# Two entries in an order-writer's clock: when a transfer may first be read, and what GpSimd's powers cost

## The chip, the cores and the metric

The kernel runs on one core of a Trainium2 chip. The metric is the device time of one execution in microseconds (us). Three runs of the kernel before took 699.75, 700.22 and 701.14 us; the median is 700.22 us.

## The reference

One decoder layer for 512 tokens of width 1024, in float32. A vector `c` gives six modulation vectors, shift, scale and gate for each of two sublayers:

```
h = x * (1 + sc1) + sh1
proj = h @ w_in                      # q, k, v (8 heads x 64), z, xBC, dt
o_attn = block-sparse causal attention(q, k, v) with ALiBi
xs, B, C = split(silu(conv4(xBC)))   # 16 heads x 64, 2 groups, state 128
dt = softplus(dt_raw + bias);  a = -exp(a_log)
y = ssd_scan(xs, dt, a, B, C) + xs * d      # chunks with cumulative sums of dt * a
y = rmsnorm_by_group(y * silu(z)) * norm_w
x = layer_norm(alpha * x + (1 + g1) * (concat(o_attn, y) @ w_out))
h = x * (1 + sc2) + sh2
u = conv3(h @ w_up);  y = (silu(u[:2816]) * u[2816:]) @ w_down
x = layer_norm(alpha * x + (1 + g2) * y)
```

The scan needs, for each head and each chunk of tokens, the matrix exp(cs[l] - cs[s]) for l >= s, where cs is the running sum of dt * a. These running sums are the "decay sums" of this document. The layer norms and the grouped norm need a power of -0.5 of a variance.

## The kernel before, in words

Tokens lie in four tiles of 128. Every float32 product is three products of a rounded part and its remainder (`mm3`, line 456): weights arrive by DMA as `raw`, ScalarE (ACT) rounds them to `wh`, VectorE (DVE) subtracts and gives `wl`. Modulation and the first product (`first`) come at the start, then the input projection (`fm` with features on the partitions, `tm` for the values with tokens on them), with the state-space scan and the attention woven in, then the output projection `po` with the first layer norm (LN1), the up projection (`up`, and from the fourth pair of tiles on a scheme of seven half-size products, `sP`), the down projection `dn` and the second layer norm (LN2).

Nothing of the order is written by hand. The work is written as some dozens of generators, called threads here. Each yields one operation, or a list of TensorE operations, or a request for a buffer, or a condition. `Order.run` (line 356) holds a model clock for each engine and each DMA queue. Again and again it asks for each thread's next operation when it could start by this clock, takes the earliest (within 0.2 us of it, on the vector engines, the one of best priority) and emits it into its engine's queue. On the chip, every engine then works through its queue in that order, and waits for what an instruction needs. The clock therefore changes nothing but the order; a wrong clock leaves engines waiting with ready work behind the waiting instruction.

Three places of the clock matter:

* `price` (line 198) gives the duration of an operation on an engine. For GpSimd's power it takes a constant and a term for each column (line 230).
* `start` (line 240) gives the earliest start: the end of each write that is read, a latency by the writing engine (`LAT`, line 237; 1.0 us for SP, which issues the DMAs), a margin for TensorE of 0.35 us, and a number `late` of the buffer, which is added only where its last writer was a DMA of SP:

```
t = max(t, w[0] + self.LAT[w[1]] + margin + (r.late if w[1] == "S" else 0.0))
```

* `emit` (line 275) moves the clocks on. A DMA of SP is issued 0.47 us (0.64 with 64 partitions) after the one before it, and lands no earlier than 0.65 us after that, plus its size over 350 GB/s or, with short runs, a larger figure; transfers follow one another.

`try_alloc` (line 146) sets `late` when it hands out a buffer, by the buffer's name.

The decay sums take this way. `dt_chain` (line 856) makes the running sums of all 16 heads, writes them transposed to DRAM (`drcs`, line 903), and negated to `ncs`. For each of eight units of two heads `ssd_decay` (line 943) then takes a buffer `csb` (three at a time) and reads 4 KB of the sums into all 128 partitions at once, 512 KB:

```
yield S.dma_start(c_.rearrange("p t h l -> p (t h l)"), bass.AP(tensor=cs_d.tensor, ...))   # 947
...
yield A.activation(er[q], c_[q, 1:, i], AF.Exp)            # 953, twice: the first use
yield G.affine_select(c_, c_, ... fill=NEG)                # 956
yield A.activation(c_[:, t, h], c_[:, t, h], AF.Exp, bias=ncs[...])   # 960, eight times
yield V.tensor_mul(q, q, b)                                # 965, twice
```

`er` is on 64 partitions each. `ssd_out` (line 997) multiplies the result with the values on TensorE (`py`). Beside it `ssd_state` (line 969) makes the chunk states: a product `pst`, a copy of its first chunk to `st` on ACT or DVE, updates of `st` on DVE, and a product `pyo`, which is multiplied with `er`. Convolutions of the input (`conv4`, line 815) use ACT too, with a tanh written to `th`.

The powers are GpSimd's (POOL's) `tensor_tensor` with `half`, which holds -0.5: one of four columns for each of the two groups in `norm` (line 1210, tile `ss`), and one of a single column for each token tile of LN1 and of LN2 in `ln_stats` (line 1248, tile `mv`). In LN1 (`ln1`, line 1269) DVE then makes the bias, ACT and DVE write one half each of the normalised rows `XN`, and TensorE transposes these (`pt`). LN2's last tile is `ln2` with `last` set (line 1474).

Of the kernel before, what the change touches and what calls it, by code (L numbers as in the profile page):

```python
# [32 lines left out]
def _n(ap):  # L33
    n = 1
    for d in ap.shape[1:]:
        n *= d
    return n
# [70 lines left out]
class Order:  # L108
# [37 lines left out]
    def try_alloc(self, a):  # L146
        if a.after:
            if self.due(a) > self.time:
                return None
            a.after = ()  # L150
        pool, slots = self.pools[a.cls]
        group = a.group or a.cls
        if self.used.get(group, 0) >= self.quota.get(group, 1000):
            return None
        free = [s for s in slots if s["free"]]
        if not free:
            return None
        s = min(free, key=lambda q: q["end"])
        t = pool.tile(a.shape, a.dt, name=self.name(a.name), tag=s["tag"], bufs=1)
        s["free"] = False  # L160
        self.used[group] = self.used.get(group, 0) + 1
        self.regs[t.tensor.name] = Region(s["end"])
        self.regs[t.tensor.name].psum = a.cls == "ps"
        self.regs[t.tensor.name].whole = a.name == "sP"
        self.regs[t.tensor.name].late = 2.0 if a.name == "ad" else 0.0
        self.owner[t.tensor.name] = (s, group)
        return t

# [29 lines left out]
    def price(self, eng, fn, outs, ins, kw):  # L198
        n = max(_n(a) for a in outs + ins)
        if eng == "PE":  # L200
            if fn == "transpose":
                return 0.109
            lhs, rhs = ins[0], ins[1]
            cols, m = _n(rhs), _n(lhs)
            if lhs.dtype == F32R:
                return max(0.111 if m > 64 else 0.056, cols * 0.0004557)
            return max(0.222, cols * 0.00168) if m > 64 else 0.000834 * cols
        if eng == "GD":
            run = 512 if any(a.tensor.name.startswith("in_") for a in ins) else 2048
            return 4 * P * _n(outs[0]) / run * (0.02 + 9.0e-5 * run) / 16  # L210
        if eng == "S":
            size = 4
            for d in outs[0].shape:
                size *= d
            ap = [a.ap for a in outs + ins if a.tensor.name.startswith(("in_", "out_", "dr"))][-1]
            run = 4 * (ap[-1][1] if ap[-1][0] == 1 else 1)
            return max(size / 3.5e5, size / run * (0.007 + 4.0e-5 * run) / 16)
        ptr = sum(1 for a in ins if _n(a) == 1)
        if eng == "A":
            return 0.04 + 0.00093 * n + (0.06 + 0.07 * ptr if ptr else 0) + (0.09 if "accum_out" in kw else 0)  # L220
        if eng == "V":
            if fn == "reciprocal":
                return 0.065 + 0.0065 * n
            if fn in ("tensor_scalar", "tensor_copy") and all(a.space != PSUM for a in ins):
                return 0.065 + 0.00052 * n + (0.06 if ptr else 0)
            return 0.065 + 0.00104 * n + (0.06 if ptr else 0)
        if fn in ("affine_select", "memset", "iota"):
            return 0.06 + 0.001 * n + (0.5 if n > 512 else 0)
        if kw.get("op") == OP.pow:
            return 0.3 + 0.164 * n  # L230
        if fn == "scalar_tensor_tensor":
            return 0.1 + 0.00139 * n
        if fn in ("tensor_scalar", "tensor_copy"):
            return 0.12 + 0.0034 * n
        return 0.1 + 0.0022 * n
# [1624 lines left out]
```

## Time and profile before

| | |
|---|---|
| timed runs, us | 699.75, 700.22, 701.14 |
| median, us | 700.22 |
| span of the profiled execution, first to last instruction, us | 698.5 |
| TensorE busy, of the span | 684.3 us, 98% |
| VectorE, ScalarE, GpSimd busy | 87%, 56%, 15% |
| mean granted TensorE clock | 0.997 |
| moved by DMA | 116.64 MB |

The profile gives no other time of the profiled execution than its span; the median of the timed runs is 1.7 us more. In the rows of a timeline stand the start, the duration, the engine, the operation with what it writes and reads, and in brackets how long the engine had been idle before and what ended that. Nearly all operations carry line 309, where the order-writer emits them, so rows are told apart by their tiles. A timed busy share of TensorE includes the tails of pipelined products; the distance from one start to the next tells more.

### The profile page before, as it was taken

To read this page: it belongs to the slowest core of one execution; us is meant where nothing else is said; L and a number is where in the kernel's file an instruction comes from. 1 tells how busy PE (TensorE), PEld (TensorE's weight loads), DVE (VectorE), ACT (ScalarE), POOL (GpSimd) and SP (SyncE) were. 2 spreads that over 40 slices of the span, in tenths; PEclk is the share of its full clock that TensorE was granted. 3 is DMA by queue.
4 is the path that set the end of the run, shared out by engine and by line. 5 is a ranking of instruction groups with operands and counts; after the bars stand their busy time and mean duration, and the time that the engine had idled before them with its cause. 6 is when DMAs were issued, how large, how long until landed. Compare 5 with 4: busy or idle time off the path is not lost.

```text
span 698.5 us, 11597 instructions
## 1 busy us (share of the span) xinstructions
PE 684.3 (98%) x4305; PEld 598.0 (86%) x4305; DVE 607.3 (87%) x1119; ACT 387.8 (56%) x739; POOL 103.4 (15%) x109
## 2 busy tenths in 40 slices
PE   8999999999999999999999999999999999999995
PEld 7787877888888888887898999999999998888885
DVE  5888989899999999889999999999999997357646
ACT  2437568845667545313886777777777776111300
POOL 0010021101000000000121121112222005910023
PEclk9999999999999999999999999999999999999998
DMA  8997074134455626677493787877897576232202
GB/s 269 308 289 241 16 215 149 37 87 126 120 178 160 237 92 212 246 275 256 137 233 73 174 200 165 187 174 167 189 204 173 130 255 220 94 108 70 91 30 92
DMA packets 134924, 116.64 MB, mean 167 GB/s; under 512 B 4565, under 2 KB 113489, under 8 KB 134867
## 3 DMA queue, kind: packets, MB, share of 16 engines
q1 hardware_dynamic: 122099, 105.93, 49.4%
q0 software_dynamic: 12768, 9.96, 9.8%
q8 instruction: 34, 0.56, 0.3%
q14 instruction: 23, 0.19, 0.1%
HBM read 106.66 MB, written 4.23 MB: 159 GB/s over the span
## 4 chain that ended last, share of the span: by engine, by line
PE 85%; DVE 6%; DMA 4%; SPq 3%; ACT 1%; issue 1%; POOL 0%; DVEq 0%; ACTq 0%; POOLq 0%
PE sP L309 27%; PE fm L309 18%; PE dn L309 18%; PE po L309 7%; PE first L309 3%; SPq L309 3%; PE tm L309 2%; PE psS L309 2%; PE pov L309 1%; PE pT L309 1%; PE py L309 1%; DMA csb<-drcs 1%; PE pyo L309 1%; PE up L309 1%; DMA raw<-in_ffn_up_w_dram 1%
## 5 line engine op out<-in xcount | busy, mean ns | idle before, releaser
L309 PE MATMUL sP<-ts,wq 128*128 128x256 f32 x912 | 113.9, 281 | 0.0
L309 DVE TENSOR_TENSOR wl<-raw,wh 128x1024 fp32r<-128x1024 f32 x64 | 80.6, 1265 | 36.6 <-ACT wh L309 36.1
L309 ACT ACTIVATE wh<-raw 128x1024 fp32r<-128x1024 f32 x64 | 67.3, 1055 | 78.0 <-PE dn L309 31.1
L309 PEld LDWEIGHTS sP<-ts,wq 128*128 128x128 f32 x912 | 110.4, 189 | 0.0
L309 PE MATMUL dn<-wh,mid 128*128 128x512 f32 (+1 forms) x356 | 102.7, 371 | 0.0
L309 PE MATMUL sP<-h2h,wq 128*128 128x256 f32 x456 | 87.2, 281 | 0.0
L309 PEld LDWEIGHTS dn<-wh,mid 128*128 128x128 f32 x356 | 64.7, 188 | 12.6
L309 PEld LDWEIGHTS sP<-h2h,wq 128*128 128x128 f32 x456 | 72.7, 189 | 0.0
L309 PE MATMUL fm<-hh,wh 128*128 128x512 f32 x176 | 72.6, 412 | 0.0
L309 PE MATMUL fm<-hh,wl 128*128 128x512 f32 x176 | 69.4, 394 | 0.0
L309 PE MATMUL fm<-hl,wh 128*128 128x512 f32 x176 | 69.4, 394 | 0.0
L309 PE MATMUL dn<-wl,mid 128*128 128x512 f32 (+1 forms) x178 | 66.1, 372 | 0.0
L309 PE MATMUL sP<-h2l,wq 128*128 128x256 f32 x228 | 64.0, 281 | 0.0
L309 DVE TENSOR_TENSOR wq<-raw,wq 128x512 fp32r<-128x512 f32 x76 | 50.8, 686 | 0.7
L309 ACT ACTIVATE wq<-raw 128x512 fp32r<-128x512 f32 x76 | 45.3, 623 | 0.0
L309 ACT ACTIVATE c<-sP 128x256 f32<-128x256 f32 x76 | 29.0, 382 | 28.5 <-PE sP L309 28.2
L309 PEld LDWEIGHTS sP<-h2l,wq 128*128 128x128 f32 x228 | 43.1, 189 | 0.1
L309 PE MATMUL po<-wh,os 128*128 128x512 f32 x128 | 42.1, 396 | 0.0
L309 PEld LDWEIGHTS fm<-hh,wl 128*128 128x128 f32 x176 | 33.1, 188 | 7.7
L309 PEld LDWEIGHTS fm<-hh,wh 128*128 128x128 f32 x176 | 33.2, 189 | 7.0 <-issue 0.7
L309 DVE TENSOR_TENSOR wq<-sw,wq 128x512 fp32r<-128x512 f32 x57 | 38.8, 684 | 0.0
L309 PEld LDWEIGHTS dn<-wl,mid 128*128 128x128 f32 x178 | 33.5, 188 | 6.2
(264 smaller groups left out, 1489.9 us busy)
## 6 DMA issues: line engine op xcount, KB each, us to landing
raw<-in_ffn_up_w_dram SPq DMA_DIRECT2D x44, 512.0 KB, 4.5
raw<-in_mix_in_w_dram SPq DMA_DIRECT2D x26, 512.0 KB, 5.8
ad<-in_ada_w_dram SPq DMA_DIRECT2D x24, 512.0 KB, 3.9
raw<-in_ffn_down_w_dram SPq DMA_DIRECT2D x22, 512.0 KB, 3.7
aw<-in_ada_w_dram SPq DMA_DIRECT2D x32, 256.0 KB, 5.8
raw<-in_mix_out_w_dram SPq DMA_DIRECT2D x12, 512.0 KB, 4.0
sw<-in_ffn_up_w_dram SPq DMA_DIRECT2D x19, 256.0 KB, 4.9
raw<-raw POOLq DMA_DIRECT2D x19, 256.0 KB, 4.6
```

What stands on the lines that cost most here:

```text
L309: getattr(self.hw[op.eng], op.fn)(*op.args, **op.kw)
```

## The change

In `try_alloc`, buffers named `csb` get a `late` of 3.0 us; so far only `ad` had one, 2.0 us. In `price`, a power on GpSimd with n columns costs 0.78 + 0.1 n us instead of 0.3 + 0.164 n: for one column 0.88 instead of 0.464, for four 1.18 instead of 0.956.

```diff
-        self.regs[t.tensor.name].late = 2.0 if a.name == "ad" else 0.0
+        self.regs[t.tensor.name].late = {"ad": 2.0, "csb": 3.0}.get(a.name, 0.0)
...
         if kw.get("op") == OP.pow:
-            return 0.3 + 0.164 * n
+            return 0.78 + 0.1 * n
```

No operation, buffer or transfer is added or taken away. What changes is the order in which the queues are filled.

## The prediction

> **What bounds the kernel now.** I read the engine shares first, then busy time by stage, then what TensorE waited for, and last the timelines around the two edited places.
>
> ```profile
> span 698.5 us, 11597 instructions
> PE 684.3 (98%) x4305; PEld 598.0 (86%) x4305; DVE 607.3 (87%) x1119; ACT 387.8 (56%) x739; POOL 103.4 (15%) x109
> ```
>
> TensorE is busy for 98% of the span, so a new order of the same work can gain only what TensorE still waits. By stage (the window, its length, then busy time of PE, PEld, DVE, ACT and POOL with counts, granted clock, DMA share, GB/s):
>
> ```profile
> 60.00:90.00 30.00, 30.00 (x149) 23.65 (x148) 28.11 (x59) 16.32 (x30) 0.00 (x0) 1.00 0.20 58
> 90.00:126.00 36.00, 34.66 (x223) 28.21 (x222) 31.14 (x56) 27.71 (x68) 7.36 (x6) 1.00 0.63 192
> 126.00:268.00 142.00, 141.99 (x845) 116.47 (x844) 134.72 (x322) 86.50 (x191) 8.38 (x14) 1.00 0.41 127
> 268.00:343.00 75.00, 74.28 (x358) 60.12 (x357) 66.27 (x111) 29.66 (x49) 3.28 (x4) 1.00 0.67 232
> 343.00:381.00 38.00, 37.95 (x273) 35.36 (x272) 36.24 (x57) 30.09 (x55) 7.67 (x7) 1.00 0.77 180
> 381.00:568.00 187.00, 187.00 (x1584) 187.00 (x1584) 185.44 (x301) 138.47 (x265) 34.99 (x32) 1.00 0.78 177
> 568.00:691.00 123.00, 123.00 (x597) 102.56 (x595) 75.27 (x93) 32.72 (x43) 36.17 (x25) 1.00 0.34 114
> ```
>
> Between 60 and 691 us TensorE is idle for 1.34 us in 90 to 126, for 0.72 us in 268 to 343, and for 0.06 us elsewhere. The waits of the window 60 to 381 name the places (total, times, longest):
>
> ```profile
> PE pyo L309 <- ACT st L309: 0.8, 1, 0.8
> PE pt L309 <- DVE XN L309: 0.7, 2, 0.4
> PE py L309 <- issue: 0.5, 1, 0.5
> ```
>
> The first and third lie where the decay sums come back from DRAM, the second in LN1, where GpSimd raises the variance to -0.5. The change edits the planned times of just these two things. Everything before 88 us, where neither occurs, should stay as it is.
>
> **The change part by part.** No instruction and no DMA is added or removed. Only the build-time clock moves, and with it the order in each engine's queue.
>
> *The decay sums.* ACT's timeline at the first use:
>
> ```profile
> 90.92 1.05 ACT L309 ACTIVATE wh<-raw 128x1024 fp32r<-128x1024 f32 x1
> 95.51 1.07 ACT L309 ACTIVATE er<-csb 64x384 f32<-64x384 f32 x2 [3.54 <-DMA csb<-drcs]
> 96.61 0.63 ACT L309 ACTIVATE th<-Y 128x512 f32<-128x512 f32 x1
> 98.24 1.07 ACT L309 ACTIVATE er<-csb 64x384 f32<-64x384 f32 x2 [1.00 <-DMA csb<-drcs]
> 99.33 0.28 ACT L309 ACTIVATE st<-pst 128x128 f32<-128x128 f32 x1
> 99.63 1.06 ACT L309 ACTIVATE wh<-raw 128x1024 fp32r<-128x1024 f32 x1
> 100.59 1.05 ACT L309 ACTIVATE er<-csb 64x384 f32<-64x384 f32 x2
> 101.67 7.14 ACT L309 ACTIVATE csb<-csb,ncs 128x128 f32<-128x128 f32 x24
> ...
> 90.42 1.39 SPq L309 DMA_DIRECT2D csb<-drcs  x3
> ```
>
> Three transfers are issued from 90.42 us. The first is usable 95.51 - 90.42 = 5.1 us later and the second 2.73 us after it. The order's clock (lines 278 to 281 and LAT at 237) gives a free queue 0.47 + 0.65 + 1.50 + 1.0 = 3.6 us, and 1.50 us for each next one. So `er` stands in ACT's queue 1.5 us too early, or more, and ACT waits 3.54 and 1.00 us with `th` and `st` queued behind it. `st` copies a state product out of PSUM, and TensorE's `pyo` waits for it:
>
> ```profile
> 98.42 0.39 PE L309 MATMUL tm<-wh,hl 128*128 128x512 f32 x1
> 99.66 1.38 PE L309 MATMUL pyo<-CT,st 128*128 128x128 f32 x6 [0.85 <-ACT st L309]
> 100.79 0.48 PE L309 MATMUL tm<-wh,hh 128*128 128x512 f32 x1
> ...
> 151.30 0.83 PE L309 MATMUL pyo<-CT,st 128*128 128x128 f32 x6
> 151.88 0.48 PE L309 MATMUL fm<-hh,wh 128*128 128x512 f32 x1
> ```
>
> From start to start an undisturbed `pyo` takes 151.88 - 151.30 = 0.58 us and a `tm` product 0.23. Here both took 100.79 - 98.42 = 2.37 us, so 1.56 us is lost: the idle 0.85, and six products that follow the four small `st` updates on VectorE one by one. With 3.0 us added, the clock gives 6.6, 8.1 and 9.6 us after 90.42, against the trace's 5.1, 7.8 and (no wait) at most 10.2. All three then stand about where the data is, and `th` and `st` move ahead. Between nothing and 1.56 us I take **1.40**, near the upper end, because the wait that held `st` is named in the rows.
>
> The Trainium skill weighs in here: "DMA: Bandwidth & Descriptors", section "Anatomy of one DMA", fits one transfer as about 2.0 us plus bytes over 436 GB/s, an estimate of 3.2 us for these 512 KB. By that the old clock was late enough, the 3.0 us would be pure delay, and the sum would lose its 1.40. The trace has 5.1 us and a wait of 3.54, and I go by the trace.
>
> A further loss is a `py` behind VectorE's backlog:
>
> ```profile
> 110.82 0.40 PE L309 MATMUL tm<-wh,hl 128*128 128x512 f32 x1
> 111.69 1.09 PE L309 MATMUL py<-csb,xd 128*64 128x128 f32 x16 [0.47 <-issue]
> ...
> 106.23 0.40 PE L309 MATMUL tm<-wh,hl 128*128 128x512 f32 x1
> 106.56 0.66 PE L309 MATMUL py<-csb,xd 128*64 128x128 f32 x8
> ```
>
> 0.87 us from `tm` to `py`, against 0.33 at an undisturbed place: 0.54 lost. It may go with the late chain or recur elsewhere; I take half, **0.27**.
>
> What is late next: per unit two `er` (1.07 us), a GpSimd select, eight exps and two VectorE products, then `py`. They may come up to 3.0 us later in the plan. The cover is the value projection and the products after it: 126 to 268 us shows 0.01 us of TensorE idle. Its price is nothing while that lasts, and up to 3.0 us without it. The later five transfers get the 3.0 us too, but their rows show no wait for the DMA, so nothing is to be gained there.
>
> *The powers.* The clock priced one column at 0.3 + 0.164 = 0.46 us and four at 0.96; now it is 0.88 and 1.18.
>
> ```profile
> L309 POOL TENSOR_TENSOR mv<-mv,half 128x1 f32<-128x1 f32 x8 | 7.1, 886 | 137.0 <-DVE mv L309 130.6 <-ACT acch L309 6.4
> L309 POOL TENSOR_TENSOR ss<-ss,half 128x4 f32<-128x4 f32 x2 | 2.4, 1187 | 72.3 <-DVE ss L309 72.3
> ...
> 327.45 0.55 POOL L309 TENSOR_TENSOR mv<-mv,half 128x1 f32<-128x1 f32 x1 [51.72 <-DVE mv L309]
> 333.20 0.87 POOL L309 TENSOR_TENSOR mv<-mv,half 128x1 f32<-128x1 f32 x1 [5.20 <-DVE mv L309]
> ...
> 328.62 0.40 PE L309 MATMUL po<-wh,oa 128*128 128x512 f32 x1
> 329.43 1.09 PE L309 MATMUL pt<-ident,XN 128*128 128x128 f32 x8 [0.41 <-DVE XN L309]
> ...
> 334.30 0.39 PE L309 MATMUL po<-wh,os 128*128 128x512 f32 x1
> 334.99 0.30 PE L309 MATMUL pt<-ident,XN 128*128 128x128 f32 x1 [0.31 <-DVE XN L309]
> ```
>
> Means of 0.886 and 1.187 agree with the new prices. In LN1 the normalised rows `XN`, and behind them the transposes `pt`, were planned 0.42 us early. The two waits cost 0.81 + 0.69 - 2 x 0.23 = 1.04 us of TensorE. The first pow took only 0.55, so its error was 0.09; correcting 0.09 + 0.42 is worth some 0.5. I take **0.40**, between nothing and 1.04. The four-column powers are 0.22 us later behind a full TensorE: nothing. LN2's last pow comes after the last product, inside one thread whose own order can't change: nothing, and at most 0.3 either way.
>
> *New waits of the reshuffled order.* Every later choice can flip. The bounds are nothing and all of today's idle over again, 2.1 us; I take **0.30**, near the lower end, as the longest stretch with a free choice (126 to 268) shows 0.01.
>
> Sum: 1.40 + 0.27 + 0.40 - 0.30 = 1.77 us. The span goes from 698.5 to 696.7. The median of the runs, 700.22, stands 1.7 us above that one span, which I keep: **698.5 us**.
>
> **The rivals.** *All of it goes:* 1.56 + 0.54 + 1.04 = 3.1 us, 697.1. For it: these are all the waits there are. Against: it needs no new one in 600 us.
>
> *The wait only moves:* ACT still has three `er` pairs and 24 exps for the first three units, and `py` follows them; if TensorE loses there what it gains at 99 us, only the powers' share stays, 699.9. For it: from 98.24 us on ACT's rows follow one another without a gap, and the exps alone take 7.14. Against: the fill of `tm`.
>
> *Slower, VectorE becomes the bound:* its products with the decay come up to 3.0 us later, so it idles 3.0 us more in 90 to 126. From 381 to 568 it is busy 185.44 of 187 us, so a debt that gets there makes TensorE wait for split weights, less 1.56 us: 1.4 to 3.0 us, and the gain at 99 us is lost with it: 701.7 to 703.2, say 702.4. For it: 95% busy in 126 to 268. Against: VectorE still idles 7.3, 8.7 and 1.8 us in the three stages between. It decides when these are forced waits and absorb less than half of the 3.0. The selects add to it:
>
> ```profile
> L309 DVE TENSOR_TENSOR csb<-csb,sc x16: 678/684/1585, 103.0 to 168.7; 128x512 f32<-128x512 f32 x16
> L309 POOL TENSOR_SCALAR_AFFINE_SELECT csb<-csb x8: 1098/1111/2012, 96.7 to 164.2; 128x1024 f32<-128x1024 f32 x8
> ```
>
> Some take 0.9 us more than the median on both engines at once; bunched selects would give VectorE up to 3 x 0.9 us. The Trainium skill's "SBUF — State Buffer", section "Terms", says the two engines hold their shared port pair exclusively for a whole instruction; the rows agree.
>
> *It does not do what it says:* something else keeps `er` early, and ACT still waits; then this too is 699.9, and counts with the second.
>
> **How the numbers follow.** The forecast has 0.48, with its own range 697.5 to 699.4; all gone 0.10; moved or unchanged 0.24; slower 0.18. A change under 0.2%, 1.4 us here, can't be told from none. A quarter of the forecast's share lies within that, so faster is 0.36 + 0.10 = 0.46, same 0.12 + 0.24 = 0.36, slower 0.18. The range of 696.9 to 702.0 leaves out the best of the second case and the upper part of the slower one.
>
> **What would show it.** Right: the idle before the first two `er` rows is under 1 us, `th` and `st` stand ahead of them, `pyo` starts without a wait, TensorE's idle in 90 to 126 falls below 0.5 us, and `pt` waits less. Wrong: the wait for the transfer persists, or a new TensorE wait over 1 us shows anywhere, above all on weight splits after 381 us.

## The result and the profile after

The changed kernel takes 696.84 us (median of four runs, 696.55 to 697.12), beside 700.46 us for the kernel before (four runs, 699.75 to 701.14). The ratio is 0.995, with a 95% interval of 0.9936 to 0.9964: 3.6 us faster, by half a per cent. A second set of runs of the same kernel gave 0.9954 [0.9939, 0.9969]. The forecast was 698.5 us; the result lies 0.06 us below the lower end of its range and is nearest to the rival "all of it goes" (697.1).

The head of the page of the profile after, as shown for before:

```profile
span 695.4 us, 11592 instructions
PE 683.0 (98%) x4305; PEld 597.6 (86%) x4305; DVE 606.5 (87%) x1119; ACT 389.3 (56%) x739; POOL 102.1 (15%) x109
```

The profiled span is 3.1 us shorter. That execution took 697.12 us, 0.28 above its median, and the one of before 700.22, 0.24 below its median; with these the 3.1 become 3.6.

The busy time by stage, changed kernel (window, its length, then busy time of PE, PEld, DVE, ACT and POOL with counts, granted clock, DMA share, GB/s):

```profile
90.00:126.00 36.00, 36.00 (x233) 29.93 (x232) 33.60 (x58) 27.83 (x69) 8.88 (x6) 1.00 0.66 206
126.00:268.00 142.00, 141.42 (x842) 115.99 (x842) 135.72 (x326) 87.40 (x193) 7.57 (x13) 1.00 0.44 137
268.00:343.00 75.00, 75.00 (x366) 61.03 (x365) 64.17 (x110) 31.59 (x54) 3.71 (x4) 1.00 0.63 213
```

TensorE's idle time in 90 to 126 us went from 1.34 to 0, in 268 to 343 from 0.72 to 0. In 126 to 268 it rose from 0.01 to 0.58. The waits of TensorE from 60 to 381 us, changed kernel, are a single row, and there is none behind it:

```profile
PE pad L309 <- DVE mx L309: 0.5, 1, 0.5
```

ACT's timeline where the decay sums are first read, changed kernel:

```profile
91.21 1.06 ACT L309 ACTIVATE wh<-raw 128x1024 fp32r<-128x1024 f32 x1
95.62 0.63 ACT L309 ACTIVATE th<-Y 128x512 f32<-128x512 f32 x1 [3.35 <-issue]
96.16 1.04 ACT L309 ACTIVATE wh<-raw 128x1024 fp32r<-128x1024 f32 x1
97.11 0.26 ACT L309 ACTIVATE st<-pst 128x128 f32<-128x128 f32 x1
97.26 2.70 ACT L309 ACTIVATE er<-csb 64x384 f32<-64x384 f32 x5
100.65 4.79 ACT L309 ACTIVATE csb<-csb,ncs 128x128 f32<-128x128 f32 x16 [0.69 <-POOL csb L309]
105.47 0.52 ACT L309 ACTIVATE er<-csb 64x384 f32<-64x384 f32 x1
```

`th` and `st` stand ahead of `er`, and no row waits for the transfer. But ACT is idle for as long as before, 3.35 us instead of 3.54: now the row at its head is `th`, which is not ready earlier either. `st` is copied at 97.11 instead of 99.33. What follows is different too. Of ACT's timeline before, this row was not shown yet:

```profile
109.67 0.26 ACT L309 ACTIVATE st<-pst 128x128 f32<-128x128 f32 x1
```

Now there are 16 exps in one row instead of 24, and the second state copy is no longer ACT's at 109.67, behind all 24, but VectorE's, five us earlier. VectorE's timeline, changed kernel:

```profile
104.66 0.29 DVE L309 COPY st<-pst 128x128 f32<-128x128 f32 x1 [0.83 <-PE pst L309]
108.88 0.69 DVE L309 TENSOR_TENSOR xd<-pxt,dt 128x512 f32<-128x512 f32 x1 [0.71 <-PE pxt L309]
```

TensorE's timeline, changed kernel, at the two places that the prediction priced:

```profile
98.73 0.39 PE L309 MATMUL tm<-wh,hl 128*128 128x512 f32 x1
98.96 0.83 PE L309 MATMUL pyo<-CT,st 128*128 128x128 f32 x6
99.54 0.48 PE L309 MATMUL tm<-wh,hh 128*128 128x512 f32 x1
...
103.79 0.83 PE L309 MATMUL pst<-xe,sc 128*128 128x128 f32 x6
105.25 1.09 PE L309 MATMUL py<-csb,xd 128*64 128x128 f32 x16
107.17 1.09 PE L309 MATMUL py<-csb,xd 128*64 128x128 f32 x16
```

`pyo` takes its undisturbed 0.58 us (99.54 - 98.96), the second `pst` stands ahead of the first `py`, and the `py` of the first two units stand apart. Before, both followed one another and `pst` came behind them; timeline of TensorE before:

```profile
106.56 1.97 PE L309 MATMUL py<-csb,xd 128*64 128x128 f32 x32
108.46 0.94 PE L309 MATMUL pst<-xe,sc 128*128 128x128 f32 x6
```

**Where the time went.** Start to start, the first products of the stages of TensorE stand so; before:

```profile
88.79 0.40 PE L309 MATMUL tm<-wh,hh 128*128 128x512 f32 x1
122.77 0.40 PE L309 MATMUL fm<-hh,wh 128*128 128x512 f32 x1
378.80 0.28 PE L309 MATMUL sP<-h2h,wq 128*128 128x256 f32 x1
568.15 0.39 PE L309 MATMUL dn<-wh,mid 128*128 128x512 f32 x1
```

and in the changed kernel:

```profile
89.08 0.39 PE L309 MATMUL tm<-wh,hh 128*128 128x512 f32 x1
120.94 0.39 PE L309 MATMUL fm<-hh,wh 128*128 128x512 f32 x1
377.42 0.28 PE L309 MATMUL sP<-h2h,wq 128*128 128x256 f32 x1
565.08 0.39 PE L309 MATMUL dn<-wh,mid 128*128 128x512 f32 x1
```

From `tm` to `fm` 33.98 became 31.86 us, 2.12 less. From there to `sP` 256.03 became 256.48. From `sP` to `dn` 189.35 became 187.66, 1.69 less. The start gave 0.29 away (88.79 against 89.08), ahead of any row that changed place; in a second profiled execution of the changed kernel it was 88.84, so this is a difference between executions.

Since products change sides between stages, I also worked out from all matmul rows what each stage loses: for each pair of neighbouring products (by tile and width) the distance of their starts, less the usual distance of such a pair, which is the lower quartile over fourteen traces of this study. "Lost" is the sum over the stage, in us; the difference between two kernels counts, not the level.

| stage (from its first product) | before | changed | changed, again |
|---|---|---|---|
| `tm` to `fm` (89 to 122) | 6.08 | 3.96 | 3.98 |
| to `po` (to 268) | 13.38 | 14.06 | 14.04 |
| to `up`, with LN1 (to 343) | 3.31 | 2.62 | 2.39 |
| to `sP` (to 378) | 0.35 | 0.56 | 0.56 |
| `sP` (to 566) | 3.76 | 2.52 | 2.52 |
| `dn` to the end | 1.16 | 1.13 | 1.13 |

The changed kernel gains 2.1 where the decay sums are read and 0.7 to 0.9 at LN1, gives 0.7 back between them and 0.2 at `up`, and gains 1.2 in `sP`, a stage for which the prediction had no term.

### The profile page after: what moved, and what is told of

The parts are those of the page before. It is cut to its first block, busy times and chain, and to the rows that moved or that the text cites. A ratio compares the mean times of both kernels' runs of the same rounds, so it can differ in the third digit from the quotient of the medians.

```text
span 695.4 us, 11592 instructions
## 1 busy us (share of the span) xinstructions
PE 683.0 (98%) x4305; PEld 597.6 (86%) x4305; DVE 606.5 (87%) x1119; ACT 389.3 (56%) x739; POOL 102.1 (15%) x109
## 4 chain that ended last, share of the span: by engine, by line
PE 91%; DVE 4%; ACT 2%; SPq 1%; DMA 1%; issue 1%; DVEq 0%; ACTq 0%
PE sP L309 27%; PE dn L309 18%; PE fm L309 14%; PE po L309 10%; PE up L309 5%; PE first L309 4%; PE tm L309 3%; SPq L309 1%; PE pov L309 1%; PE pT L309 1%; PE py L309 1%; PE psS L309 1%; DMA wr<-in_mix_in_w_dram 1%; PE pst L309 1%; PE pad L309 1%; PE pyo L309 1%
```

## The experiments

Two theories were to be told apart. The one on record: the wait for the transfer, which holds `st` in ACT's queue, is what costs; taking it away is the gain. Its rival: that wait only moves, and the gain, where there is one, is in what else the new plan changes. Ratios are to the kernel before, on the same chip, with a 95% interval.

**The exchange alone.** The order of before, but when the queues are filled the first two pairs of `er` and the select between them are held back until the first `st` copy is emitted. Everything else keeps its place; the queues of TensorE, VectorE and GpSimd hold the same rows in the same order as before.

```diff
-        getattr(self.hw[op.eng], op.fn)(*op.args, **op.kw)
+        for o in self.swapped(op): ...emit o
+    def swapped(self, op):   # from the first er_ of ACT on:
+        # hold er_ and csb_ of ACT and GpSimd; at ACT's first st_ return [op] + held
```

> The clock and so every queue's order are those of before, with one local exchange: the first two pairs of er and the select between them are emitted behind the first copy of st, so that ACT's queue is th, st, er, er instead of er, th, er, st. Theory (the wait for the first decay transfers held the state copy, and TensorE behind it): pyo starts without its 0.85 us wait, TensorE gains 1.56 us from tm to tm there, the py at 111 us keeps its 0.54 us or part of it, and everything behind is as before: the ratio to before is 0.9978, about 1.5 us less. Rival (most of the measured gain comes from the new order of the 600 us behind this place, and this wait is hidden by something else): pyo starts earlier but the time stays within 0.5 us of before. Rival (the whole 3.6 us hang on this one wait): about 3.6 us less.

It took 700.72 us, ratio 1.0002 [0.9993, 1.0011]: no gain, and by the interval at most 0.5 us, where 1.5 were expected. ACT's timeline of this kernel:

```profile
95.52 0.63 ACT L309 ACTIVATE th<-Y 128x512 f32<-128x512 f32 x1 [3.36 <-issue]
96.93 0.28 ACT L309 ACTIVATE st<-pst 128x128 f32<-128x128 f32 x1 [0.78 <-PE pst L309]
97.10 2.15 ACT L309 ACTIVATE er<-csb 64x384 f32<-64x384 f32 x4
...
101.33 7.13 ACT L309 ACTIVATE csb<-csb,ncs 128x128 f32<-128x128 f32 x24
```

and its TensorE waits, the whole list from 60 us on:

```profile
PE py L309 <- ACT er L309: 1.1, 1, 1.1
PE pt L309 <- DVE XN L309: 0.7, 2, 0.4
PE py L309 <- DVE csb L309: 0.2, 1, 0.2
```

`st` came 2.4 us earlier than before, the wait of `pyo` is gone, and a wait of 1.1 us has come at the third unit's `py`. The exps still end at 108.5 (108.8 before). So removing the named wait is worth nothing in the old order.

**The exchange and the next one.** In the same kernel, the third unit's `xd` is also emitted ahead of the two `Y` products and the state update that stood before it in VectorE's queue.

```diff
+        # after that, in VectorE's queue: hold ops from the first reader of py_ on,
+        # until one writes xd_; return [it] + held
```

> The order of before with two local exchanges. The first is the one that moved the first state copy ahead of two er pairs and only moved TensorE's wait from 99 to 110 us (from the first tm to the first fm behind it 33.44 us, against 33.98 before). The second takes VectorE's queue at the place where the wait went: the copy xd of the third unit, which py waits for, goes ahead of two products with Y and one state update. Theory (the wrong landing left a chain of rows in the wrong order, and the wait moves along it until all of them are right): py starts 0.7 to 1.4 us sooner, tm to fm takes 32.1 to 32.8 us, and the time is 0.9 to 1.8 us below before. Rival (ACT's exps set the pace, and the wait moves on again): tm to fm stays at 33.2 us or more and the time within 0.7 us of before.

It took 699.69 us, 0.999 [0.9981, 1.0], a gain of 0.7 us by the ratio and 0.3 by the medians, at the edge of what can be told; 0.9 to 1.8 were expected. The 1.1 us of `py` have become two rows. That is the rival of the expectation: the wait moved on again:

```profile
PE py L309 <- DVE csb L309: 0.6, 2, 0.3
PE py L309 <- ACT er L309: 0.5, 1, 0.5
```

From `tm` to `fm` it needs 33.39 us, the exchange alone 33.44, before 33.98, the changed kernel 31.86. These two exchanges don't get there.

**The wait put back.** The changed kernel, but its first pair of `er` is emitted ahead of `th`, `wh` and `st` again.

```diff
+        # from the 8th th_ of ACT on: hold everything until two er_ have come; return er_, er_, held
```

> The changed kernel's order with one exchange back: ACT's first pair of er stands again at the head of the rows that use the decay sums, ahead of th, wh and st, and so waits for the transfer there as it did before. All other rows keep their order. Theory (the gain lies in the order of the whole stretch, not in which row meets the transfer's end): ACT waits 3 us or more before the first er, pyo starts 0 to 0.7 us later, and the time is within 0.7 us of the changed kernel. Rival (the wait of that one row is what cost time): 1.2 to 2.1 us above the changed kernel.

It took 697.31 us, 0.9956 [0.9942, 0.997]; the changed kernel beside it on the same chip 697.12, 0.9954. ACT's timeline of this kernel:

```profile
95.75 1.07 ACT L309 ACTIVATE er<-csb 64x384 f32<-64x384 f32 x2 [3.48 <-DMA csb<-drcs]
96.84 0.63 ACT L309 ACTIVATE th<-Y 128x512 f32<-128x512 f32 x1
97.38 1.04 ACT L309 ACTIVATE wh<-raw 128x1024 fp32r<-128x1024 f32 x1
98.33 0.26 ACT L309 ACTIVATE st<-pst 128x128 f32<-128x128 f32 x1
```

The wait for the transfer stands there as before, 3.48 us long, `st` is 1.2 us later than in the changed kernel, and `pyo` starts at 98.95 without a wait. The lost time of the stage is 4.21 instead of 3.98. So ACT's wait for the transfer as such is worth about 0.2 us, by the times and by the rows alike, and less than these runs can tell from nothing; the gain is in the rest of the stretch's order. One limit: TensorE's own wait for `st` did not come back with it, since `st` stands ahead of the second pair of `er` here. `pyo` takes 0.83 us to the next `tm` product (98.95 to 99.78) instead of 0.58, where before 1.56 us was lost. The exchange shows that ACT can stand before the transfer at almost no price, not what TensorE's wait would cost in the new order.

**The parts alone.** Each of the two edits by itself, and the 3.0 us for the first three of the eight transfers only, without and with the new price of the powers.

```diff
 csb_only:   only the line with late
 pow_only:   only the two numbers of price
 first3:     self.count3 += a.name == "csb"; ... 3.0 if a.name == "csb" and self.count3 <= 3
 first3_pow: first3 and the new price
```

> Only the 3.0 us behind the landing of the decay sums; the powers keep their old price. Theory (the decay part gives 1.4 to 2.1 us near 90 to 122 us, the powers the rest in LN1): 1.4 to 2.1 us less than before, and pt still waits 0.5 to 1.0 us in LN1. Rival (the order behind 122 us is luck that hangs on both edits): anything between 0 and 4 us less, with TensorE ahead by 1.5 to 2.1 us at 122 us all the same.

> Only the new price of GpSimd's powers. Nothing changes before the first power at 251 us, so the waits at 98 and 111 us stay as they were. Theory: pt's waits in LN1 shrink from 1.04 us to 0.5 or less, 0.4 to 1.0 us less than before. Rival (the price changes nothing that TensorE waits for): within 0.3 us of before.

> The 3.0 us for the first three decay transfers only, which are issued together and whose first use waited; the other five keep 0, and the powers their old price. Theory (only the first uses matter): at 122 us TensorE is 1.5 to 2.1 us ahead as with all eight, and the time is 1.2 to 2.5 us below before. Rival (the later five matter too, by the order of what follows): at least 1 us apart from the kernel with all eight.

> The 3.0 us for the first three transfers, and the new price of the powers. Theory (the two parts touch different places and add up): tm to fm 31.9 us, no wait of pt, 696.5 to 697.6, as the changed kernel or a little below. Rival (behind 122 us the orders are a lottery of about 1 us): anywhere from 696 to 699.

| kernel | us | ratio | lost `tm` to `fm` | to `po` | LN1 | `sP` |
|---|---|---|---|---|---|---|
| before | | 1 | 6.08 | 13.38 | 3.31 | 3.76 |
| csb_only | 698.93 | 0.9973 [0.9961, 0.9985] | 3.95 | 14.04 | 2.31 | 3.31 |
| pow_only | 699.05 | 0.9986 [0.9977, 0.9996] | 5.15 | 13.44 | 2.90 | 3.05 |
| first3 | 697.61 | 0.9959 [0.9947, 0.9971] | 3.98 | 13.87 | 2.54 | 3.26 |
| first3_pow | 697.77 | 0.9966 [0.9953, 0.9979] | 3.98 | 13.92 | 2.50 | 3.42 |

Three things follow. The first three transfers carry the whole gain from `tm` to `fm`; with the 3.0 us on all eight the kernel is not faster than with three (by the medians 1.3 us slower, with intervals that overlap). The waits of `pt` at LN1 are absent from csb_only too, which has the old price of the powers: the price is one way of removing them, not the only one. Up to 248 us the queues of csb_only hold the same rows in the same order as those of the changed kernel, so up to there the price does nothing. And the edits don't add up: the price is worth 1.0 us on the old order and nothing on top of first3. On top of csb_only, which was not on the same chip, the changed kernel is 0.2% faster (0.995 against 0.9973, intervals that just meet), and by the rows about half of that is in `sP` (3.31 to 2.52).

In the run of pow_only the order up to 251 us is that of before, yet its `pyo` shows no wait. Timeline of TensorE, pow_only:

```profile
99.25 1.38 PE L309 MATMUL pyo<-CT,st 128*128 128x128 f32 x6
100.38 0.48 PE L309 MATMUL tm<-wh,hh 128*128 128x512 f32 x1
```

The second pair of `er` did not wait there, where before it waited 1.00 us, so the transfers landed otherwise in this execution. ACT's timeline, pow_only:

```profile
97.82 1.07 ACT L309 ACTIVATE er<-csb 64x384 f32<-64x384 f32 x2
```

One and the same order loses 6.08 us in one execution and 5.15 in another.

**How late.** The added number alone, at 1.5 and 6.0 us instead of 3.0; then with the new price of the powers, at 2.5 and 3.5.

```diff
-        self.regs[t.tensor.name].late = 2.0 if a.name == "ad" else 0.0
+        self.regs[t.tensor.name].late = {"ad": 2.0, "csb": 1.5}.get(a.name, 0.0)   # 6.0, 2.5, 3.5
```

> The first use 1.5 us behind the landing, half the change's, old price of the powers. The first transfer was 1.5 us later than the clock had it, the third up to 2.1. Theory (the clock has to stand behind the data): the first er waits less than 1.5 us for its transfer but the later ones may still wait; tm to fm between 32 and 33.5 us, so less of the 2.1 us is gained than with 3.0. Rival (any reshuffle of this stretch does it): tm to fm 31.9 us, the same as with 3.0.

> The decay sums' first use 6.0 us behind the landing, twice the change's, with the old price of the powers. Theory (3.0 us is enough to stand behind the data, more only moves the units later behind a TensorE that has other work): no wait for the transfer, tm to fm 31.8 to 32.4 us as with 3.0, and a time 0.5 to 2.8 us below before. Rival (the amount matters, and too late costs as much as too early): tm to fm 33 us or more. Rival (VectorE becomes the bound): weight splits waited for after 381 us and a time above before.

> The change with 2.5 us in the place of 3.0. Theory (beyond the landing's error the amount only reshuffles what follows): TensorE loses 3.9 to 4.3 us from tm to fm as with 3.0, and the rest differs by up to 1.5 us either way, 696 to 698.5 in all. Rival (3.0 is a lucky value for all that follows): 698.5 or more.

> The change with 3.5 us in the place of 3.0. Theory and rival as for 2.5: 696 to 698.5 in all, or 698.5 and more if 3.0 is a lucky value.

| added, us | price | us | ratio |
|---|---|---|---|
| 1.5 | old | 698.77 | 0.9981 [0.997, 0.9992] |
| 3.0 (csb_only) | old | 698.93 | 0.9973 [0.9961, 0.9985] |
| 6.0 | old | 700.14 | 0.9998 [0.9987, 1.0008] |
| 2.5 | new | 697.13 | 0.995 [0.9937, 0.9963] |
| 3.0 (changed kernel, again) | new | 697.12 | 0.9954 [0.9939, 0.9969] |
| 3.5 | new | 697.85 | 0.9962 [0.995, 0.9975] |

With 1.5 us the two `er` rows behind the first still wait a little, ACT's timeline of that kernel:

```profile
97.78 1.07 ACT L309 ACTIVATE er<-csb 64x384 f32<-64x384 f32 x2
99.13 1.07 ACT L309 ACTIVATE er<-csb 64x384 f32<-64x384 f32 x2 [0.28 <-DMA csb<-drcs]
100.50 0.53 ACT L309 ACTIVATE er<-csb 64x384 f32<-64x384 f32 x1 [0.30 <-DMA csb<-drcs]
```

and the stretch loses 4.12, nearly as little as with 3.0. That profiled execution took 700.10 us, 1.3 above the median of the kernel, and `pt` waits in it as before, 0.7 us. With 6.0 the stretch loses least of all, 3.27, and the next one gives most of it back, 15.62 instead of 13.38. Its busy time there (same columns as above) and the first of its TensorE waits:

```profile
126.00:268.00 142.00, 140.70 (x838) 114.89 (x835) 133.52 (x318) 86.09 (x191) 10.18 (x14) 1.00 0.40 123
```

```profile
PE py L309 <- DVE er L309: 0.7, 1, 0.7
PE fm L309 <- DVE oa L309: 0.3, 1, 0.3
```

TensorE is idle for 1.30 us of the 142, against 0.01 before. Planned too late by this much is as dear as planned too early; between 1.5 and 3.5 us the number itself makes no difference that these intervals can tell. None of these beats the changed kernel; 2.5 us equals it.

**The same kernel again**, with its own profile.

> The changed kernel once more, unaltered, as the yardstick of this comparison. Its time was 696.8 us; within 1 us of that, 2.2 to 4.2 us below before.

697.12 us (696.46 to 698.71), 0.9954 [0.9939, 0.9969]; its stages are in the first table. The gain in `sP` came back to the hundredth.

## Why the prediction was right or wrong

Direction and places held: TensorE's idle time fell in just the two stretches that the prediction named, `th` and `st` went ahead of `er`, `pyo` starts without a wait, `pt` doesn't wait. The size was too small by half: 3.6 us for a forecast of 1.77, and the time lies just outside the stated range. The rival "all of it goes" came nearest by its number alone: it counted three waits and no new one, while 0.9 us of new waits and 1.24 us of gain in `sP`, neither in its terms, largely cancel here.

| step | taken | bounds | profile after |
|---|---|---|---|
| state copy and `pyo`, and `py` behind VectorE | 1.40 + 0.27 | 0 to 2.10 | 2.12 |
| the powers at LN1 | 0.40 | 0 to 1.04 | 0.69, again 0.92 |
| new waits | -0.30 | -2.1 to 0 | -0.68 to `po`, -0.21 to `sP` |
| `sP` | none | none | 1.24 |
| start, ahead of the change | none | none | -0.29, again -0.05 |

The rows of the last column add up to 2.87 of the 3.11 us; the rest is 0.03 at the end and differences in the usual distances, since some products have other neighbours now.

**The state copy: right sum, wrong reason.** The step took 1.40 "because the wait that held `st` is named in the rows". The exchange removed that wait and gained nothing, and putting it back cost some 0.2 us. The rows show why the name misled: with `er` out of the way ACT is idle for 3.35 us all the same, since the `Y` that `th` reads isn't there earlier. VectorE's timeline before:

```profile
93.72 1.53 DVE L309 SCALAR_TENSOR_TENSOR Y<-fm,prm,Y 128x510 f32<-128x510 f32 x2
```

`Y` ends at 95.25 and `th` started at 96.61, so the transfer cost `th` at most 1.4 us, not 3.5. And behind it stood what the rival "the wait only moves" named, 24 exps and the `py` that need them. In the old order that rival is right, measured: 1.0002. What made the gain is the new plan behind this point, which the prediction had only as a risk ("Every later choice can flip", at a cost of 0.30): 16 exps in a row, the second state copy with VectorE, `pst` ahead of `py`, and more work of TensorE ahead of the next unit. Between the `py` of the second and of the third unit stand 6 `tm` products before and in the exchange, 21 in the changed kernel. Which of these four carries the 2.1 us wasn't separated. That the size of this step came near is luck.

**The `py` behind VectorE's backlog** was taken at half, 0.27 of 0.54. It went whole: the stage loses 2.12 less, all that the prediction had found at the two places (1.56 + 0.54), and neither loss is left in the changed kernel's rows.

**The landing.** The prediction set the trace's 5.1 us for the first transfer against an estimate of 3.2 us from the Trainium skill's "DMA: Bandwidth & Descriptors", section "Anatomy of one DMA", by which the 3.0 us would be pure delay and gain nothing at this place. The heading of that section of the Trainium skill gives the fit for transfers that GpSimd issues, and these are issued by SP, so it was no close match. Here 1.5 us gains 0.19% and the first three transfers' 3.0 us 0.41%; the measurement goes with the trace. It doesn't prove the landing as the cause, since the kernel with the wait put back is as fast.

**The powers.** 0.40 for 0.69 to 0.92: mis-sized, not misplaced. But the step gave the gain to the price alone, and csb_only shows the same waits gone without it. With the price alone the waits at `pt` shrink from 0.7 to 0.4 and the kernel gains 1.0 us, part of it in `sP`. The four-column powers, put at nothing, do move rows: the first that change place in pow_only stand at 252.5 us, just behind the first of these powers. What that is worth wasn't separated.

**New waits** were 0.9 in all instead of 0.3, of which the one named row, `pad` behind VectorE's `mx`, is 0.5. The step that failed is its reason, that "the longest stretch with a free choice (126 to 268) shows 0.01": that stretch is where most of it came. What a full stretch shows is that the old order fits there, not that a new one will.

**`sP`** had no term, since "a new order of the same work can gain only what TensorE still waits", and TensorE showed no wait there. That step failed. The busy time shows TensorE without a gap in both kernels, but not with the same number of products; before:

```profile
381.00:565.00 184.00, 184.00 (x1559) 184.00 (x1559) 182.44 (x298) 135.75 (x261) 34.99 (x32) 1.00 0.78 177
```

and in the changed kernel:

```profile
381.00:565.00 184.00, 184.00 (x1570) 184.00 (x1569) 182.65 (x298) 138.40 (x263) 34.99 (x32) 1.00 0.76 175
```

Eleven products more in the same 184 us, at 184 / 1570 = 0.117 us each 1.3 us. A further 0.46 us of the 1.69 is work that only changed its place: the last two `pad` products stood at 379.83 inside `sP` before and stand at 342.10 now. Timeline of TensorE, before:

```profile
379.83 0.39 PE L309 MATMUL pad<-acch,ones_r 128*128 128x512 f32 x1
```

and in the changed kernel:

```profile
342.10 0.40 PE L309 MATMUL pad<-acch,ones_r 128*128 128x512 f32 x1
```

The gain isn't in a few stalls: from 8 us behind the first `sP` product on, neighbouring `sP` products start 118.2 ns apart on average before and 117.4 ns in the changed kernel, which makes some 1.2 us over about 1530 of them.

**The rival "the wait only moves"** was priced with a slip: 700.22 - 0.40 is 699.8, not 699.9.

**The slower rival** asked for VectorE to come into debt. Its idle time in 90 to 126 fell instead of rising by 3.0 (36 - 31.14 = 4.86 before, 36 - 33.60 = 2.40 after). With 6.0 us the loss that it feared did come, but between 122 and 268 and not on the weight splits behind 381.

## What to carry to other kernels

The length of a named wait is not its price: look at what the engine could have done in its place and at what stands next in the chain, and where it can be tried, take the wait away alone before paying for it. Where a planner's clock differs from the trace, correcting the clock can gain more than moving the row that waits, because everything behind it is planned anew; by the same token a part of such a result, here more than 1 us of the 3.6, belongs to the new order elsewhere and wasn't to be forecast from the place of the edit. A stage that shows an engine busy for 100% can still hold time, here 0.7%: compare the count of its instructions over the same time.

## What the runs showed of the hardware

**A full TensorE at different paces.** `sP` is the same 1596 products in all kernels, and no wait is named there from 381 us on in before, in csb_only, first3 or the changed kernel. In 381 to 565 us before completes 1559 products, the exchange alone (same order there) 1559, csb_only 1560, pow_only and first3 1563, the wait put back 1569 and the changed kernel 1570. In the second profile of the changed kernel `dn` begins at 564.60, inside this window, and the count is 1567; the distance of neighbours leaves no such doubt. From 8 us behind the first `sP` product on it is 118.2 to 118.3 ns on average in before, the exchange alone and the exchange with the next one, 117.4 to 117.5 ns in the changed kernel, in its second profile and with the wait put back, and between these or at the upper end in the others (118.1 in csb_only, 117.8 in first3, 118.0 with 3.5 us and the new price). The granted clock is shown as 1.00 throughout. So the pace follows the order and comes back with it; what in the order makes it was not found. ACT's load in this stretch is no ready answer: 138.40 us busy in the changed kernel and 137.93 in first3, with 7 products between them.

**Transfers land differently from one execution to the next.** With one order of the queues the second decay transfer held ACT for 1.00 us in one execution and not at all in another, and the stretch lost 6.08 and 5.15 us. A term that is read from one execution has here an error of 0.9 us, more than half of the 1.56 that was taken from it.
